# A two-block transformer kernel: first norm's squares moved to ScalarE on a natural copy of the input, residual squares one tile behind, two sets of products moved behind the first tiles

## The chip, the cores and the metric

The kernel runs on one core of a Trainium2 chip. The time is the device time of one execution in microseconds; the time of a kernel is the median of its runs. Beside the runs stands one profiled execution, from whose trace all rows below are taken.

## The reference, cut to what matters

256 tokens of width 2048 in fp32 go through a first block (a double attention, then a gated feed-forward part) and a second block (an attention layer, then a retention layer).

```python
def rms_norm(x, g):
    xf = x.astype(jnp.float32)
    y = xf * lax.rsqrt(jnp.mean(xf * xf, axis=-1, keepdims=True) + NORM_EPS)
    return (y * g.astype(jnp.float32)).astype(x.dtype)

# first block
u = rms_norm(h, norm_pre_mix)
proj = u @ w_in                      # 256 x 2048 @ 2048 x 8512
...
mixed = (g_sb * y_sb + g_mla * y_mla) @ w_out
h = h + rms_norm(mixed, norm_post_mix)
gu = rms_norm(h, norm_pre_ffn) @ w_gate_up
h = h + rms_norm((silu(g) * up) @ w_down, norm_post_ffn)
# second block, layer 0: attention with normed and rotated q and k
q = apply_rope(rms_norm_2(q, q_gain), cos, sin) * (A_HEAD_DIM ** -0.5)
k = apply_rope(rms_norm_2(k, k_gain), cos, sin)
p = softmax(q @ k.T); o = p @ v; y = (o * silu(gate)) @ w_out
# then a residual layer norm, the retention layer and a second residual layer norm
```

## The kernel before, in words

**Units.** All weights stream through one loop (`run`, line 226). A unit is one tile of weights of 256 x 512: SP's queue loads it into `raw` (five buffers, four units ahead in the order written), ScalarE copies it into the high part `whi`, VectorE subtracts to give the low part `wlo` (four buffers, split three units ahead), and TensorE uses both with the high and low parts of the activations, three products for each pair. `gemm_t` makes results transposed (features on partitions), `gemm_n` makes them natural (tokens on partitions), 512 columns a group, in two of the four PSUM banks of the pool `psg`. The pool hands its banks out in turn, so a group takes the banks of the group before the last. Every engine runs its own instructions in the order in which the program writes them.

**Background stages.** Work that is not a product of the stream (norms, attention heads, transposes) is cut into stages and put into tasks (`bg_add`). After each unit `bg_step` runs one stage that is due, or up to two in the attention layer (`rate` 2); at most two tasks are taken from the waiting list, `urgent` ones go ahead of them, `gap` is the least number of units between two stages, and `after` names a group that has to be finished first.

**The start.** The input comes transposed (`xs`, eight loads of two chunks between the first weight loads). `x_split` makes `u`'s high and low parts for two chunks ahead of each of the first eight weight splits, and has GpSimd square the chunks and add the squares up (`sq0`). After the first group, `r0_stages` sums `sq0` over partitions with TensorE (`token_sums`), computes the reciprocal root in small steps on GpSimd (`rms_bg`), spreads it over partitions and evacuates the first group (`evac_first`).

**The norm turns.** Between the output projection `w_out` and the feed-forward part the step `enter_ffn` ends one norm and begins the next matrix. The last group's two accumulators are read by a square on ScalarE (`sum_wout`) and by `put_wout`, two VectorE multiplications for each half of the tokens. `enter` turns the first tile of the new activations (transposes on TensorE, high part, low part); `two_groups` then interleaves the first two groups of the new matrix (unit order a0 a1 b0 b1 a2 a3 b2 b3 and so on), holds a0's products back until a1, and puts the seven other tile turns (`turn_now`) and the sums that they need (`turn_make`) behind certain units. The background task "h" meanwhile forms the residual `y` tile by tile on VectorE and squares each tile on ScalarE (`rest`). `enter_attn` does the same between `w_down` and the attention layer, with `put_down` (one VectorE multiplication for each half, in SBUF) and without squares. `b1` is the fourth unit of the interleaved order; its split is written in a0's place, and a2's behind a1.

**Attention.** `evac_qk` puts up a task "prep" for each group of four query heads: squares, rotation on VectorE and GpSimd, and a last stage `s3` of transposes and splits into `qT`. The heads' tasks (`att_head`) wait for the end of that task; their first stage multiplies `qT` with `kT`.

Of the kernel before, what the change touches and what calls it, by code (L numbers as in the profile page):

```python
# [10 lines left out]
F32 = mybir.dt.float32  # L11
# [3 lines left out]
ALU = mybir.AluOpType  # L15
AX = mybir.AxisListType

P = 128
S = 256
D = 2048  # L20
# [39 lines left out]
def tile_two_blocks(ctx: ExitStack, tc: tile.TileContext, a, out):  # L60
    nc = tc.nc
    pe, act, dve, pool = nc.tensor, nc.scalar, nc.vector, nc.gpsimd
# [3 lines left out]
    mp = ctx.enter_context(tc.tile_pool(name="main", bufs=1))  # L66
# [17 lines left out]
    def bbank():  # L84
        return psb.tile([P, 512], F32, tag="b", name="b")
# [23 lines left out]
    def mul(o, x, y, eng=None):  # L109
        tt(o, x, y, ALU.mult, eng)  # L110

    def add(o, x, y, eng=None):
        tt(o, x, y, ALU.add, eng)
# [10 lines left out]
    def stt(o, x, s, y, op0, op1):  # L124
        dve.scalar_tensor_tensor(out=o, in0=x, scalar=s, in1=y, op0=op0, op1=op1)  # L125
# [25 lines left out]
    def bg_add(group, stages, gap=2, after=None, delay=0, urgent=False):  # L151
        t = Task(group, stages, gap, after, clock[0] + delay)
        if urgent:
            active.insert(0, t)
        else:
            waiting.append(t)
# [66 lines left out]
    before_load, before_split = {}, {}  # L223
# [223 lines left out]
    def cols(g):  # L447
        return slice(g * 512, (g + 1) * 512)
# [6 lines left out]
    def square_sum(junk, x, acc):  # L455
        act.activation(out=junk, in_=x, func=AF.Square, accum_out=acc)  # L456
# [39 lines left out]
    def enter(high_on, chain, rest):  # L496


        new_u()
        tr, high, low = turning["fs"][0, 0]  # L500
        tr()
        high(high_on)
        chain()
        turning["make"](0, 1)
        low()
        for f in rest:
            f()
# [10 lines left out]
    def token_sums(ps, col, tiles, start=True, stop=True):  # L518

        for i, t in enumerate(tiles):  # L520
            for tb in range(2):
                mm(ps[:, col + tb:col + tb + 1], t[:, tb * P:(tb + 1) * P], ones[:, 0:1],
                   start and i == 0 and tb == 0, stop and i == len(tiles) - 1)

    def small(name, w=2, bufs=2):
        return mp.tile([P, w], F32, tag="sm_" + name, name=name, bufs=bufs)
# [16 lines left out]
    def rms_bg(key, get_ps, n, dst):  # L543

        st = {}

        def row():
            v, t = small("v"), small("t")
            st["r"] = small("r", bufs=6)
            ts(v, get_ps()[:, 0:2], 1.0 / n, ALU.mult, NORM_EPS, ALU.add)  # L550
            rsqrt_bg(st["r"], v, t)

        def wide():
            st["d"] = diag(st["r"], 1.0, "gate" if key == "kv" else "sqt")

        def use():
            o = bbank()
            spread(o, 0, st["d"])
            dst(key, st["r"], o[:, 0:S])
        return [row, nop, wide, use]  # L560
# [20 lines left out]
    p1 = open_phase("p1")  # L581
    xs = p1.tile([P, KD, S], F32, tag="c", name="xs")
# [4 lines left out]
    ifr = p1.tile([64, 64], F32, tag="ifr", name="ifr")[:, 0:2]  # L587
    nc.scalar.dma_start(out=cv, in_=a["cv"])
    pool.memset(f32(wz), 0.0)
    sq0 = p1.tile([P, 2, S], F32, tag="gate", name="sq0")  # L590

    copy(small("root"), f32(wz)[:, 0:2])
    warm(22)
# [12 lines left out]
        nc.sync.dma_start(out=kp, in_=a["kc"][:, 2 * P:7 * P])  # L606
    before_load[9] = const_load

    def x_split(c):
        def f():  # L610
            for k in (c, c + 1):
                copy(U[0][:, k, :], xs[:, k, :], scale=vec("pre_mix", k))
                stt(U[1][:, k, :], xs[:, k, :], vec("pre_mix", k), f32(U[0][:, k, :]), ALU.mult, ALU.subtract)
            if c == 0:
                mul(sq0, xs[:, 0:2, :], xs[:, 0:2, :], pool)
            else:
                s2 = p1.tile([P, 2, S], F32, tag="sqt", name="sqt")
                mul(s2, xs[:, c:c + 2, :], xs[:, c:c + 2, :], pool)
                add(sq0, sq0, s2, pool)
        return f  # L620
    for i in range(8):
        before_split[i] = x_split(2 * i)
# [6 lines left out]
        rows[key], bcast[key] = r, b  # L629

    def r0_stages(evac):
        st = {}

        def sums():
            st["ps"] = bbank()
            token_sums(st["ps"], 0, [sq0[:, 0, :], sq0[:, 1, :]])
        return [sums] + rms_bg("x", lambda: st["ps"], D, to_bcast) + [evac]


    tabs = {}  # L640
# [453 lines left out]
    fin = {}  # L1094
# [23 lines left out]
    def put_wout(g, tb, p):  # L1118
        y = fin["y"][:, tb, cols(g)]
        mul(y, p, fin["post_mix"][:, cols(g)])  # L1120
        mul(fin["yg"][tb][:, cols(g)], y, fin["pre_ffn"][:, cols(g)], pool if g < 3 else dve)
# [22 lines left out]
    def rms_last(tb):  # L1144
        v = small("v1", 1)
        stt(v, fin["ss"][:, 4 * tb + 3:4 * tb + 4], 1.0 / D, fin["s3"][:, tb:tb + 1], ALU.mult, ALU.add)
        rstd(fin["r"][:, tb:tb + 1], v)
# [16 lines left out]
    for g in range(4):  # L1164
        gemm_n(a["w_out"], KD, g * 512, 512, u_rhs,
               lambda ps, g=g: [evac_wout(g, tb, p) for tb, p in enumerate(ps)],
# [1 line left out]
    at_unit(len(units) - 2, before_end)  # L1168

    def enter_ffn():  # L1170
        enter(dve, lambda: rms_last(1), [lambda tb=tb: put_wout(3, tb, fin.pop(("p", tb))) for tb in range(2)])
        fin["h"], fin["ss2"] = fin["y"], small("ss", 8)

        def rest(c, tb):
            def f():
                y = fin["y"][:, tb, cols(c)]
                stt(y, y, fin["r"][:, tb:tb + 1], fin["x"][:, tb, cols(c)], ALU.mult, ALU.add)
                junk = p1.tile([P, 512], F32, tag="sqt", name="sqh")
                square_sum(junk, y, fin["ss2"][:, 4 * tb + c:4 * tb + c + 1])
            return f  # L1180
        bg_add("h", [nop] + [rest(c, tb) for c in range(4) for tb in range(2)], gap=1)

    step(enter_ffn, norm=True)


# [80 lines left out]
    def put_down(g, tb):  # L1266
        y = ffn["acc"][:, tb, cols(g)]
        mul(y, y, fin["post_ffn"][:, cols(g)], pool if g < 3 else dve)
# [31 lines left out]
    at_unit(len(units) - 2, before_end)  # L1300

    def enter_attn():
        enter(dve, lambda: rms_last(1), [lambda tb=tb: put_down(3, tb) for tb in range(2)])

    step(enter_attn, norm=True)

# [23 lines left out]
    def evac_qk(n, g):  # L1330
        def evac(ps):
            if not at:
                start_attn()
            p3 = at["p"]
            raw = p3.tile([P, 2, 512], F32, tag="raw", name="qkraw", bufs=2)
            for tb in range(2):
                copy(raw[:, tb, :], ps[tb])
            st = {}
            tab = at["tab"][n]

            def s1():
                sq = p3.tile([P, 2, 512], F32, tag="qsq", name="qsq")
                act.activation(out=sq, in_=raw, func=AF.Square)
                v, r, t = small("v8", 8), small("r8", 8), small("t8", 8)
                dve.tensor_reduce(out=v, in_=sq.rearrange("p a (h d) -> p (a h) d", d=P), axis=AX.X, op=ALU.add)
                ts(v, v, 1.0 / P, ALU.mult, NORM_EPS, ALU.add)
                rsqrt_bg(r, v, t)
                st["r"] = r

            def s2(tb):  # L1350
                def fn():
                    if tb == 0:
                        st["t"] = p3.tile([P, 2, 512], F32, tag="qsq", name="qt2")
                    t = st["t"]
                    q4 = raw[:, tb, :].rearrange("p (h d) -> p h d", d=P)
                    mul(q4, q4, st["r"][:, 4 * tb:4 * tb + 4, None].to_broadcast([P, 4, P]))
                    for qt in range(2):
                        def qv(x, which):
                            return x[:, tb, :].rearrange("p (h f w d) -> p h f w d", h=4, f=2, w=2)[:, :, :, which, :]
                        sn = tab[:, 1, tb, :].rearrange("p (f w d) -> p f w d", f=2, w=2)[:, :, qt, :]  # L1360
                        mul(qv(t, qt), qv(raw, 1 - qt), sn[:, None, :, :].to_broadcast([P, 4, 2, 32]))
                    mul(q4, q4, tab[:, 0, tb, None, :].to_broadcast([P, 4, P]), pool)
                    add(raw[:, tb, :], raw[:, tb, :], t[:, tb, :], pool)
                return fn

            def s3():
                dst = p3.tile([P, 2, 4, S], F32R, tag=n + "T", name=n + "T", bufs=2 if n == "q" else 1)
                for j in range(2):
                    o = bbank()
                    for i in range(4):  # L1370
                        h, tb = 2 * j + i // 2, i % 2
                        pe.transpose(out=o[:, i * P:(i + 1) * P], in_=raw[:, tb, h * P:(h + 1) * P], identity=ident)
                    split_psum(dst[:, 0, 2 * j:2 * j + 2, :], dst[:, 1, 2 * j:2 * j + 2, :], split2(o))
                at[n, g] = dst
            wait = [nop, nop] if n == "q" else [nop] * 6
            bg_add("prep%s%d" % (n, g), [s1, nop, s2(0), s2(1), nop, nop] + wait + [s3], gap=1, urgent=True)
        return evac

    def evac_av(ps):
# [427 lines left out]
```

## Time and profile before

| | us |
|---|---|
| median of three runs | 2552.85 |
| lowest and highest | 2552.61, 2554.2 |
| profiled execution, its own time | 2553.11 |
| its span in the trace | 2551.4 |

The profiled execution lies 0.26 us above the median, and 1.7 us of it lie outside the span. TensorE is busy in almost the whole span, so what matters is where it stands still and where its clock is not at full speed. A row of a timeline gives the start, the duration, the engine, the line of the kernel (often that of a helper, so that the tile's name says more), the operation and tiles, the count, and in brackets the engine's idle time before it with the instruction that ended that time.

### The profile page before, as it was taken

The numbers are of one execution on the slowest core, as the hardware profiler recorded it, in microseconds if no ns is written. First come the engines' busy times: TensorE is split into PE (matmuls) and PEld (weight loads), VectorE is DVE, ScalarE is ACT, GpSimd is POOL, SyncE is SP. The second block draws the span as 40 slices with busy tenths as digits, with TensorE's granted clock in tenths as the row PEclk, the third lists the DMA queues.
The fourth block names the chain that finished last, engine by engine and source line by source line (L and its number), as shares of the span: only waits on it lengthen the run. The fifth ranks groups of instructions, "written<-read, shape, count | busy, mean of one in ns | idle before, by whom it ended". The sixth has DMA issues, their size and how long they took to land.

```text
span 2551.4 us, 36111 instructions
## 1 busy us (share of the span) xinstructions
PE 2496.5 (98%) x14332; PEld 2181.9 (86%) x14332; DVE 1518.1 (60%) x1794; ACT 1191.9 (47%) x1478; POOL 237.6 (9%) x348
## 2 busy tenths in 40 slices
PE   8999999999899999999999999999999999999997
PEld 8999999998678888888888788887989898898786
DVE  7756666556655454444555676766775656565545
ACT  4565554444444444444444455543444454454332
POOL 4012000002000000000000031112010110102000
PEclk9999999999999999999999999999999999999998
DMA  7555556656466666666656555455756556665763
GB/s 234 175 162 165 167 163 197 227 179 196 144 189 185 191 188 190 195 191 190 186 184 199 156 186 153 149 192 172 227 163 183 167 180 182 178 184 154 261 192 120
DMA packets 248890, 465.49 MB, mean 182 GB/s; under 512 B 21328, under 2 KB 31888, under 8 KB 247696
## 3 DMA queue, kind: packets, MB, share of 16 engines
q1 hardware_dynamic: 244736, 447.28, 57.8%
q0 software_dynamic: 2688, 13.63, 1.4%
q8 instruction: 112, 1.84, 0.3%
q10 hardware_dynamic: 1296, 2.27, 0.2%
q14 instruction: 58, 0.48, 0.1%
HBM read 458.92 MB, written 4.19 MB: 182 GB/s over the span
## 4 chain that ended last, share of the span: by engine, by line
PE 88%; DVE 6%; ACT 2%; issue 2%; DMA 1%; POOL 1%; SPq 0%; ACTq 0%; DVEq 0%; POOLq 0%
PE g L101 83%; PE b L101 4%; DVE wlo L107 2%; ACT whi L104 1%; DMA raw<-in_ret_w_out_dram 1%; POOL t L107 1%; DVE u L107 0%; DVE h L125 0%; PE b L1239 0%; DMA raw<-in_w_in_dram 0%; POOL t L433 0%; PE b L466 0%; DVE y L125 0%; DVE qkraw L107 0%; PE b L1661 0%
## 5 line engine op out<-in xcount | busy, mean ns | idle before, releaser
L107 DVE TENSOR_TENSOR wlo<-raw,whi 128x1024 fp32r<-128x1024 f32 (+2 forms) x849 | 1061.6, 1259 | 790.6 <-ACT whi L104 786.0
L104 ACT ACTIVATE whi<-raw 128x1024 fp32r<-128x1024 f32 (+2 forms) x852 | 887.2, 1050 | 869.7 <-PE g L101 825.6
L101 PE MATMUL g<-whi,u 128*128 128x512 f32 x3200 | 1013.3, 393 | 11.9 <-DVE u L107 4.7
L101 PEld LDWEIGHTS g<-whi,u 128*128 128x128 f32 x3200 | 602.5, 189 | 141.1 <-DVE u L107 7.6
L101 PE MATMUL g<-wlo,u 128*128 128x512 f32 x1600 | 626.0, 391 | 2.1 <-DVE wlo L107 2.0
L101 PE MATMUL g<-u,whi 128*128 128x256 f32 x3424 | 601.2, 280 | 1.3 <-ACT whi L104 1.2
L101 PEld LDWEIGHTS g<-u,whi 128*128 128x128 f32 x3424 | 520.3, 188 | 2.5 <-ACT whi L104 1.7
L101 PE MATMUL g<-u,wlo 128*128 128x256 f32 x1712 | 476.8, 279 | 8.0 <-DVE wlo L107 8.0
L101 PEld LDWEIGHTS g<-wlo,u 128*128 128x128 f32 x1600 | 302.1, 189 | 64.0 <-DVE wlo L107 3.2
L101 PEld LDWEIGHTS g<-u,wlo 128*128 128x128 f32 x1712 | 322.2, 188 | 10.2 <-DVE wlo L107 10.2
L101 PE MATMUL g<-whi,mh 128*128 128x512 f32 x352 | 139.0, 395 | 0.0
L101 PE MATMUL g<-whi,ml 128*128 128x512 f32 x352 | 137.0, 392 | 0.0
L101 PE MATMUL g<-wlo,mh 128*128 128x512 f32 x352 | 136.7, 388 | 0.0
L101 PE MATMUL g<-wlo,roh 128*128 128x512 f32 x256 | 100.6, 393 | 1.7 <-DVE wlo L107 1.7
L101 PE MATMUL g<-whi,roh 128*128 128x512 f32 x256 | 99.9, 390 | 0.1
L101 PE MATMUL g<-whi,rol 128*128 128x512 f32 x256 | 98.5, 394 | 0.0
L107 POOL TENSOR_TENSOR t<-r 128x2 f32<-128x2 f32 (+1 forms) x51 | 22.0, 431 | 633.5 <-DVE r L122 630.9
L101 PEld LDWEIGHTS g<-whi,ml 128*128 128x128 f32 x352 | 66.1, 188 | 15.4
L101 PEld LDWEIGHTS g<-wlo,mh 128*128 128x128 f32 x352 | 66.1, 188 | 14.6
L101 PEld LDWEIGHTS g<-whi,mh 128*128 128x128 f32 x352 | 66.2, 188 | 13.1
L107 POOL TENSOR_TENSOR dacc<-dacc,post_ffn 128x512 f32<-128x512 f32 x6 | 7.7, 1300 | 657.6 <-ACT sqd L456 657.6
L101 PEld LDWEIGHTS g<-wlo,roh 128*128 128x128 f32 x256 | 48.0, 188 | 13.8 <-DVE wlo L107 2.8
(315 smaller groups left out, 2221.3 us busy)
## 6 DMA issues: line engine op xcount, KB each, us to landing
raw<-in_ret_w_in_dram SPq DMA_DIRECT2D x192, 512.0 KB, 4.3
raw<-in_w_gate_up_dram SPq DMA_DIRECT2D x176, 512.0 KB, 3.7
raw<-in_w_in_dram SPq DMA_DIRECT2D x128, 512.0 KB, 4.5
raw<-in_w_down_dram SPq DMA_DIRECT2D x88, 512.0 KB, 4.5
raw<-in_attn_w_in_dram SPq DMA_DIRECT2D x80, 512.0 KB, 3.6
raw<-in_ret_w_out_dram SPq DMA_DIRECT2D x64, 512.0 KB, 4.6
raw<-in_w_out_dram SPq DMA_DIRECT2D x32, 512.0 KB, 4.4
raw<-in_attn_w_out_dram SPq DMA_DIRECT2D x32, 512.0 KB, 4.5
```

The lines of the kernel that those rows point to most:

```text
L101: pe.matmul(out=o, lhsT=l, rhs=r, start=start, stop=stop, skip_group_check=True)
L104: act.activation(out=o, in_=i, func=AF.Copy, **k)
L107: (eng or dve).tensor_tensor(out=o, in0=x, in1=y, op=op)
```

## The change

The first norm's squares are taken from a natural copy of the input (`x0`, 2 MB, tokens on partitions), which GpSimd's queue loads, by two ScalarE instructions that square and add up a row of 2048 (stages 1 and 2 of `r0_stages`, which becomes one stage longer); GpSimd's squares and sums in `x_split` and TensorE's `token_sums` go. In `enter_ffn` the four multiplications of `put_wout` for the last chunk leave the step and become the first two stages of the task "h"; in the stages after them the square of a residual tile is written one stage behind the tile. In `enter_attn` the two multiplications of `put_down` for the last chunk become a task of their own, behind units a1 and b0. In `evac_qk` each prep task gets an empty last stage.

```diff
--- before.py
+++ after.py
@@ -587,7 +587,8 @@
     ifr = p1.tile([64, 64], F32, tag="ifr", name="ifr")[:, 0:2]
     nc.scalar.dma_start(out=cv, in_=a["cv"])
     pool.memset(f32(wz), 0.0)
-    sq0 = p1.tile([P, 2, S], F32, tag="gate", name="sq0")
+    x0 = mp.tile([P, 2, D], F32, tag="x", name="x0")
+    ss0 = small("ss0")
 
     copy(small("root"), f32(wz)[:, 0:2])
     warm(22)
@@ -606,17 +607,15 @@
         nc.sync.dma_start(out=kp, in_=a["kc"][:, 2 * P:7 * P])
     before_load[9] = const_load
 
+    def x0_load():
+        pool.dma_start(out=x0, in_=a["x"].rearrange("(b p) c -> p b c", p=P))
+    before_load[8] = x0_load
+
     def x_split(c):
         def f():
             for k in (c, c + 1):
                 copy(U[0][:, k, :], xs[:, k, :], scale=vec("pre_mix", k))
                 stt(U[1][:, k, :], xs[:, k, :], vec("pre_mix", k), f32(U[0][:, k, :]), ALU.mult, ALU.subtract)
-            if c == 0:
-                mul(sq0, xs[:, 0:2, :], xs[:, 0:2, :], pool)
-            else:
-                s2 = p1.tile([P, 2, S], F32, tag="sqt", name="sqt")
-                mul(s2, xs[:, c:c + 2, :], xs[:, c:c + 2, :], pool)
-                add(sq0, sq0, s2, pool)
         return f
     for i in range(8):
         before_split[i] = x_split(2 * i)
@@ -629,12 +628,9 @@
         rows[key], bcast[key] = r, b
 
     def r0_stages(evac):
-        st = {}
-
-        def sums():
-            st["ps"] = bbank()
-            token_sums(st["ps"], 0, [sq0[:, 0, :], sq0[:, 1, :]])
-        return [sums] + rms_bg("x", lambda: st["ps"], D, to_bcast) + [evac]
+        def sums(tb):
+            return lambda: square_sum(x0[:, tb, :], x0[:, tb, :], ss0[:, tb:tb + 1])
+        return [sums(0), sums(1)] + rms_bg("x", lambda: ss0, D, to_bcast) + [evac]
 
 
     tabs = {}
@@ -1168,17 +1164,25 @@
     at_unit(len(units) - 2, before_end)
 
     def enter_ffn():
-        enter(dve, lambda: rms_last(1), [lambda tb=tb: put_wout(3, tb, fin.pop(("p", tb))) for tb in range(2)])
+        enter(dve, lambda: rms_last(1), [])
         fin["h"], fin["ss2"] = fin["y"], small("ss", 8)
 
-        def rest(c, tb):
+        items = [(c, tb) for c in range(4) for tb in range(2)]
+
+        def rest(i):
+
             def f():
-                y = fin["y"][:, tb, cols(c)]
-                stt(y, y, fin["r"][:, tb:tb + 1], fin["x"][:, tb, cols(c)], ALU.mult, ALU.add)
-                junk = p1.tile([P, 512], F32, tag="sqt", name="sqh")
-                square_sum(junk, y, fin["ss2"][:, 4 * tb + c:4 * tb + c + 1])
+                if i < 8:
+                    c, tb = items[i]
+                    y = fin["y"][:, tb, cols(c)]
+                    stt(y, y, fin["r"][:, tb:tb + 1], fin["x"][:, tb, cols(c)], ALU.mult, ALU.add)
+                if i:
+                    c, tb = items[i - 1]
+                    junk = p1.tile([P, 512], F32, tag="sqt", name="sqh")
+                    square_sum(junk, fin["y"][:, tb, cols(c)], fin["ss2"][:, 4 * tb + c:4 * tb + c + 1])
             return f
-        bg_add("h", [nop] + [rest(c, tb) for c in range(4) for tb in range(2)], gap=1)
+        puts = [lambda tb=tb: put_wout(3, tb, fin.pop(("p", tb))) for tb in range(2)]
+        bg_add("h", puts + [rest(i) for i in range(9)], gap=1)
 
     step(enter_ffn, norm=True)
 
@@ -1300,7 +1304,8 @@
     at_unit(len(units) - 2, before_end)
 
     def enter_attn():
-        enter(dve, lambda: rms_last(1), [lambda tb=tb: put_down(3, tb) for tb in range(2)])
+        enter(dve, lambda: rms_last(1), [])
+        bg_add("put", [nop] + [lambda tb=tb: put_down(3, tb) for tb in range(2)], gap=1)
 
     step(enter_attn, norm=True)
 
@@ -1372,8 +1377,8 @@
                         pe.transpose(out=o[:, i * P:(i + 1) * P], in_=raw[:, tb, h * P:(h + 1) * P], identity=ident)
                     split_psum(dst[:, 0, 2 * j:2 * j + 2, :], dst[:, 1, 2 * j:2 * j + 2, :], split2(o))
                 at[n, g] = dst
-            wait = [nop, nop] if n == "q" else [nop] * 6
-            bg_add("prep%s%d" % (n, g), [s1, nop, s2(0), s2(1), nop, nop] + wait + [s3], gap=1, urgent=True)
+            wait = [nop] * (2 if n == "q" else 6)
+            bg_add("prep%s%d" % (n, g), [s1, nop, s2(0), s2(1), nop, nop] + wait + [s3, nop], gap=1, urgent=True)
         return evac
 
     def evac_av(ps):
```

## Rows read from the trace of the kernel before

**Rows 1.** The page's part 1: busy time, share, instructions of each engine.

```profile
PE 2496.5 (98%) x14332; PEld 2181.9 (86%) x14332; DVE 1518.1 (60%) x1794; ACT 1191.9 (47%) x1478; POOL 237.6 (9%) x348
```

**Rows 2.** Waits of TensorE over the whole span: us in total, times, longest.

```profile
PE g L101 <- DVE wlo L107: 12.5, 13, 3.0
...
PE b L101 <- ACT qT L104: 2.8, 4, 0.8
...
PE b L101 <- DVE qT L107: 0.9, 4, 0.2
```

**Rows 3.** Windows of the start: us, five engines' busy time, granted clock, DMA, GB/s.

```profile
0.00:14.00 14.00, 8.55 (x54) 7.95 (x55) 8.54 (x7) 9.39 (x16) 8.94 (x11) 1.00 0.88 309
14.00:18.00 4.00, 3.83 (x22) 3.53 (x20) 4.00 (x4) 3.18 (x6) 3.76 (x4) 0.57 0.98 359
18.00:30.00 12.00, 8.71 (x71) 8.31 (x72) 12.00 (x9) 3.88 (x7) 9.92 (x7) 1.00 0.59 169
```

**Rows 4.** Timeline of the start, TensorE.

```profile
6.64 2.10 PE L101 MATMUL g<-u,whi 128*128 128x256 f32 x16 [1.19 <-ACT whi L104]
...
13.29 0.39 PE L101 MATMUL g<-u,wlo 128*128 128x256 f32 x1 [3.00 <-DVE wlo L107]
...
41.04 0.95 PE L101 MATMUL b<-kc,sq 128*128 128x1 f32 x8
```

**Rows 5.** Timeline of the start, VectorE.

```profile
13.16 2.68 DVE L125 SCALAR_TENSOR_TENSOR u<-xs,cv,u 128x256 fp32r<-128x256 f32 x2
...
30.13 0.87 DVE L125 SCALAR_TENSOR_TENSOR u<-xs,cv,u 128x256 fp32r<-128x256 f32 x2
30.92 1.21 DVE L107 TENSOR_TENSOR wlo<-raw,whi 128x1024 fp32r<-128x1024 f32 x1
```

**Rows 6.** Timeline of the start, ScalarE.

```profile
5.53 1.06 ACT L104 ACTIVATE whi<-raw 128x1024 fp32r<-128x1024 f32 x1 [0.65 <-DMA raw<-in_w_in_dram]
...
38.40 1.06 ACT L104 ACTIVATE whi<-raw 128x1024 fp32r<-128x1024 f32 x1 [1.65 <-PE g L101]
```

**Rows 7.** DMA, 436.5 to 447: queues (packets, MB, share); issue (KB, us to landing).

```profile
q0 software_dynamic: 348, 2.72, 62.6%
q1 hardware_dynamic: 593, 1.15, 35.3%
...
xres<-in_x_dram POOLq DMA_DIRECT2D x1, 2048.0 KB, 9.5
```

**Rows 8.** ScalarE's copies of input chunks: ns min/median/max, first and last start.

```profile
L104 ACT ACTIVATE u<-xs,cv x16: 492/492/508, 4.0 to 22.1; 128x256 fp32r<-128x256 f32 x16
```

**Rows 9.** Windows of two norm turns, columns as in rows 3.

```profile
662.24:710.81 48.57, 39.52 (x169) 29.92 (x170) 32.63 (x42) 21.59 (x36) 2.91 (x1) 0.96 0.42 120
1416.91:1454.69 37.78, 37.65 (x169) 30.45 (x170) 27.15 (x32) 16.68 (x20) 2.88 (x1) 0.95 0.57 167
```

**Rows 10.** Timeline of the norm before the feed-forward block, TensorE.

```profile
662.24 0.47 PE L101 MATMUL g<-whi,u 128*128 128x512 f32 x1 [0.88 <-DVE v L125]
...
670.00 2.50 PE L101 MATMUL g<-whi,u 128*128 128x512 f32 x5 [2.25 <-DVE u L107]
```

**Rows 11.** Timeline of the same norm, VectorE, then ScalarE.

```profile
664.60 0.68 DVE L107 TENSOR_TENSOR y<-g,post_mix 128x512 f32<-128x512 f32 x1
665.32 1.57 DVE L107 TENSOR_TENSOR yg<-y,pre_ffn 128x512 f32<-128x512 f32 x1
...
668.13 1.22 DVE L107 TENSOR_TENSOR wlo<-raw,whi 128x1024 fp32r<-128x1024 f32 x1
669.26 0.68 DVE L107 TENSOR_TENSOR u<-b,u 128x512 fp32r<-128x512 f32 x1
...
671.26 1.06 ACT L104 ACTIVATE whi<-raw 128x1024 fp32r<-128x1024 f32 x1 [5.83 <-PE g L101]
```

**Rows 12.** Waits in that norm's turn, 664 to 708, all engines.

```profile
ACT sqh L456 <- DVE y L125: 17.8, 8, 3.3
```

**Rows 13.** Timeline of one attention group, TensorE.

```profile
1616.00 0.38 PE L101 MATMUL g<-u,wlo 128*128 128x256 f32 x1 [0.54 <-DVE wlo L107]
```

## The prediction

> **What bounds the kernel.** I read the page first. TensorE is busy for 98% of the span [rows 1], so the time is its matrix work plus the places where it stands still or runs at half clock; no other engine is near its limit over the whole. A faster ScalarE or GpSimd is worth nothing by itself. The second view is TensorE's waits over the whole span. The ones that the change can touch are its waits for `wlo`, most of them in the start, and for `qT` in the attention [rows 2]. The third view is the table of windows over the start, then the timelines of the start, of the norm before the feed-forward block and of one attention group, and the DMA view at the one place where a 2 MB load on GpSimd's queue already runs beside the weights.
>
> **The start: what goes.** From 4 to 28 us GpSimd squares and adds almost without a pause, and VectorE is full from 14 to 30 [rows 3]. VectorE's two products for a pair of chunks take 2.68 us while GpSimd works and 0.87 when it has stopped [rows 5]. With the subtraction (1.21 undisturbed) a unit needs 2.1 us of VectorE without GpSimd and over 4 with it, against TensorE's 2.72 for a unit (ScalarE's 1.06 and its 1.65 of waiting for TensorE to give a buffer back [rows 6]). So in the start VectorE sets the pace, and TensorE waits: 3.0 us at 13.29 alone [rows 4]. It then runs at a granted clock of 0.57 from 14 to 18 us [rows 3], which lies near the lower level of 1.2 GHz, after standing still before 13.29; that costs 4 x 0.43 = 1.7 us. With GpSimd's 15 instructions gone, VectorE needs less than TensorE.
>
> The pace is then TensorE's, and the question is when it begins. Before, the first weights were there at 5.53 and the products began at 6.64 [rows 4, 6]; 16 of unit 0's 24 products took 2.10, so it ended near 9.75, and unit 8 at 41.04, where the eight token sums begin [rows 4]. If nothing else changed, unit 8 would end at 9.75 + 8 x 2.72 = 31.5, 9.5 us earlier. The token sums go too: 0.95 us with the overlap into the next product, of which I count 0.8.
>
> **The start: what comes.** The 2 MB of `x0` are written into the program at the ninth load, but GpSimd's queue holds nothing in front of them except the first memset, and their buffer has no earlier reader. They start at about 1.1 us, in the window in which the DMA engines are already full (share 0.88 over 0 to 14 with its first 2 us empty, 0.98 from 14 to 18) [rows 3]. The nearest rows are those of the other 2 MB load on this queue: 9.5 us to landing, with 62.6% of the engines' time against 35.3% for the weights' queue beside it [rows 7]. With about 390 GB/s for the whole, the weights' queue gets 0.138 MB/us while `x0` flows, from about 2.7 to 10.6 us. The first input chunks (0.26 MB) are through by then, the 0.52 MB of the first weights need 3.8 us, and with 1 us to the semaphore (before: 0.79 MB from 2.0 on, seen at 5.5) they are there at 7.5. TensorE begins at 8.6, takes 3.1 us for unit 0, and has stood still from about 5.5 on, longer than before 13.29; I charge the same 1.7 us of half clock. Unit 0 ends at 13.4. The data of unit 1 (1.57 MB in all) are complete near 12.2 and split at 14.5, so it loses 1.0. Unit 8 ends at 14.4 + 21.8 = 36.2 instead of 41.04: 4.8, and with the token sums 5.6 us. Bounds: if all of `x0` goes ahead of the first weights, these land near 13, unit 8 ends at 40.6, and 1.2 us are left; if `x0` hinders nothing it is 9.5 + 0.8 = 10.3.
>
> The Trainium skill, "DMA: Bandwidth & Descriptors", section "Queues, rings and completion order", says that an engine alternates between the queues that have work, a whole packet at a time, which speaks against this load. The trace's shares, 62.6 to 35.3, are milder than a strict alternation of its packets would make them; by that rule the sum would be 15.8 us, by the shares 17.7. What alternation would do here stands among the rivals, from rows.
>
> ScalarE pays two squares of 2048. From 492 ns for 256 [rows 8] and 1.06 us for 1024 [rows 6] I get 0.74 ns an element, so 1.8 us each, 2.0 with reading the sum. They stand in units 8 and 9, where ScalarE waits 1.65 us for TensorE in every unit [rows 6]; 0.35 us is too much each time, and the next `whi` behind them is late by 0.7 us at most. Splits run three units ahead (8.2 us), so nobody waits: 0. The chain has one stage more, so the first group is evacuated behind unit 14 instead of 13; its banks are wanted at unit 16, one unit remains, and the cost is 0. If that cover went, each us of lateness would cost one.
>
> **The norm before the feed-forward block.** The two turns have the same transposes and the same kind of products. From the first use of the new activations to the last transposes the one takes 48.57 us and TensorE is busy for 39.52; the other, which has no squares in its background task, takes 37.78 and is busy for 37.65 [rows 9]. So 10.8 us are there to be had. 2.25 of them are one wait for the low part of tile (0,1) [rows 10]: in front of it VectorE does the four multiplications for the last chunk, from 664.60 to about 668.1 [rows 11]. The rest is a chain between two engines: in each of eight units ScalarE's square waits for VectorE's residual tile (17.8 us in all [rows 12]), the `whi` stands behind the square, `wlo` waits for that `whi`, and the next tile comes behind `wlo`. With the square one stage behind its tile, ScalarE no longer waits; VectorE's unit (1.22 + 0.68 + 0.74 for the residual) fits into TensorE's.
>
> The change doesn't take all of it. Written as the first stage of "h", `put_wout` of the first half is still in front of the low part (a0's stage comes before a1's turn). VectorE then does b1's `wlo` (1.22, about 0.9 longer because GpSimd's subtraction of the step disturbs one instruction, as it now makes 1.57 of a 0.68 [rows 11]), two multiplications and the low part: ready near 668.6 instead of 669.9, so 0.9 us of the wait stay. `put_wout` of the second half goes behind a2's `wlo`, and this is a new wait: its first multiplication frees the PSUM bank that b0 wants for its second half of tokens. TensorE would resume at 668.65, use a0's `whi` for the last time at 669.1; ScalarE's a2 `whi` starts 0.34 later (now 1.26 after 670.00, with two products at half clock [rows 10, 11]), and 1.06 + 1.22 + 0.68 follow: the bank is free at 672.5. TensorE wants it at 668.65 + 4 x 0.23 + 6 x 0.23 = 670.9: it stands 1.6 us, with all later products behind it. New length: 37.78, less 0.28 for that turn's own small wait at its low part, plus 0.9 + 1.6 = 40.0; gain 8.6 us. Bounds: 10.8 if neither wait comes; 4.5 if both come, the clock halves again behind them (1.7) and a third of the chain's waits stays (2.4).
>
> **The attention turn.** Two multiplications (0.68 each) leave VectorE's way ahead of the same low part. TensorE is idle for 0.13 us in this whole turn [rows 9], with another 0.15 hidden in the modelled ends. They touch no PSUM, and land behind units in which VectorE has room. 0.3 us, from 0 to 0.6.
>
> **The attention heads.** TensorE waits 2.8 + 0.9 us, eight times in four groups, for `qT` [rows 2]: the first head's scores run in the same unit as the splits that they need. The empty last stage keeps the group pending, so they run a unit later. Each group's heads end one unit later; the last low part of all is then forced ahead of the products for chunks 12 and 13, while its own is used a unit later: 0. But a head's scores now share a unit with the next group's square and reduction, and in that stretch TensorE already waits 0.54 us for `wlo` [rows 13], in three groups. I take 3.7 - 0.5 = 3.2 us; bounds 0.7 (three waits longer by 1 us) and 5.3 (those go too).
>
> **Sum.** 5.6 + 8.6 + 0.3 + 3.2 = 17.7 us. Against the profiled execution: 2553.11 - 17.7 = 2535.4; against the median, which lies 0.26 lower, 2535.2.
>
> **Rivals, and how the numbers follow.** 0.2% is 5.1 us, about what a measurement of this kernel can tell from no change.
>
> The sum as it stands has a chance of 0.40.
>
> Strict alternation of packets in the start: the rows give 2.72 MB in 348 packets and 1.15 MB in 593 [rows 7], 7.8 and 1.9 KB, so `x0` would take four fifths. The first weights would need 6.7 us instead of 3.8 and unit 1 no longer waits: the start gives 3.7, the time is 2537.1. Against it stand the shares measured; but there the weights' queue was not full all the time. 0.17.
>
> The norm's turn keeps its standstill: the bank's wait and 1.7 us of half clock behind it, with some of the chain: gain there 4.9, time 2538.9. 0.18.
>
> The prep stage doesn't do what it should: the wait for `qT` comes back as waits for `wlo`, gain 0.7 there, time 2537.7. 0.13.
>
> `x0` is hidden wholly: 2530.5. 0.07.
>
> Slower: ScalarE takes its work in order, so a square of `x0` that waits for its data holds every later `whi`. It is reached near 33 us; with 8.2 us of splits ahead, each us of landing after about 41 costs one. The load would have to land after 59 to undo the 17.7, and after 64 to make the kernel slower by 0.2% (2558). By rows 7 it lands near 10.6. 0.02. Several terms failing at once, so that under 5.1 us remain: 0.03.
>
> Faster 0.95, same 0.03, slower 0.02. The ends of the terms add up to 6.4 and 27.2 us; all at one end is unlikely. The range leaves about 2 in 10 out: 2528 to 2544.
>
> **What would show it.** In the start: no GpSimd work, VectorE's pairs at 0.9, the first products at 8 to 10 us, unit 8 at its end near 36. In the norm's turn: squares that wait for nothing, a wait of about 1.6 us in b0 released by the multiplication on VectorE, 40 us in all. In the attention: no wait for `qT`. The prediction is wrong if the first weights land after 10 us, if the two turns stay over 4 us apart, or if waits for `wlo` grow in the attention.

## The result, and the profile after

The kernel after takes 2524.55 us (median of 4 runs, 2523.39 to 2526.17) against 2553.32 for the kernel before on the same chip (4 runs, 2552.61 to 2554.2): ratio 0.9887, 95% interval 0.9875 to 0.99, a gain of 28.8 us. Forecast were 17.7 us and 2535.2, with a range of 2528 to 2544. The direction was right, the gain was 11 us larger than the sum, and the time lies below the range.

The waits of TensorE over the whole span of the kernel after, columns as in [rows 2]:

```profile
PE g L101 <- ACT whi L104: 6.5, 3, 4.9
PE g L101 <- DVE wlo L107: 4.5, 7, 1.4
...
PE g L101 <- DVE u L107: 2.3, 2, 1.7
...
PE b L466 <- DVE z L125: 1.6, 1, 1.6
```

No wait for `qT` is left, and the waits for `wlo` fell from 12.5 us in 13 places to 4.5 in 7 [rows 2]. A new one stands at the top: 4.9 us for a `whi` of ScalarE. It lies in the start, as the windows show (columns as in [rows 3]):

```profile
0.00:14.00 14.00, 8.15 (x46) 7.65 (x46) 3.00 (x5) 4.74 (x8) 1.39 (x6) 0.98 0.87 321
14.00:18.00 4.00, 2.80 (x11) 2.51 (x12) 3.29 (x5) 3.77 (x7) 0.00 (x0) 0.50 1.07 400
18.00:30.00 12.00, 12.00 (x96) 12.00 (x95) 9.85 (x15) 8.95 (x14) 0.00 (x0) 0.91 1.06 395
```

GpSimd hardly works in the start and VectorE is no longer full, as forecast. But from 14 to 18 us the granted clock is 0.50, the lower of the two levels (1.2 of 2.4 GHz), all the time, and 0.91 from 18 to 30. The timeline of TensorE says where that comes from:

```profile
6.71 2.15 PE L101 MATMUL g<-u,whi 128*128 128x256 f32 x16 [0.48 <-ACT whi L104]
...
14.73 0.80 PE L101 MATMUL g<-u,whi 128*128 128x256 f32 x2 [4.93 <-ACT whi L104]
15.99 0.58 PE L101 MATMUL g<-u,wlo 128*128 128x256 f32 x1 [0.46 <-DVE wlo L107]
```

Unit 0 begins at 6.71, as early as before (6.64, [rows 4]); unit 1 waits 4.93 us for its data, and TensorE comes out of that standstill at half clock. The DMA view from 5 to 10 us names the cause (packets, MB, share of the 16 engines, then the load of `x0`, issued by 1.4 us, with its time to landing in the view from 0 to 12):

```profile
q0 software_dynamic: 215, 1.76, 87.6%
q1 hardware_dynamic: 212, 0.22, 12.5%
```

```profile
x<-in_x_dram POOLq DMA_DIRECT2D x1, 2048.0 KB, 11.0
```

The two queues pass the same number of packets, 215 and 212. Those of `x0` carry 8.2 KB each (1.76 MB by 215), those of the input chunks on the weights' queue 1.0 KB, so the weights' queue gets an eighth of the engines' time. The Trainium skill, "DMA: Bandwidth & Descriptors", section "Queues, rings and completion order", says that an engine alternates between its queues by whole packets; these rows agree (215 to 212).

The windows of the two norm turns, from the first use of the new activations to the last transposes, as in [rows 9]:

```profile
655.51:694.82 39.31, 36.46 (x169) 29.21 (x169) 32.78 (x42) 21.75 (x36) 2.91 (x1) 1.00 0.54 158
1398.91:1436.22 37.31, 37.31 (x169) 30.41 (x169) 27.07 (x32) 16.68 (x20) 2.90 (x1) 0.95 0.57 170
```

The first was 48.57 us and is 39.31, forecast 40.0; the second was 37.78 and is 37.31. Both waits that the working named are there, together nearly at their size (1.65 and 1.19 for 0.9 and 1.6), and no half clock follows them (granted 1.00):

```profile
662.67 1.43 PE L101 MATMUL g<-whi,u 128*128 128x512 f32 x5 [1.65 <-DVE u L107]
...
666.42 0.50 PE L101 MATMUL g<-whi,u 128*128 128x512 f32 x1 [1.19 <-DVE y L107]
```

**What no term names.** I matched the matmuls of the two traces in their order and took the difference of their starts, the lead of the kernel after (and, further down, of the other runs, always against the kernel before). It is 1.4 us at 230 us; it grows by 5.3 us from there to the norm's turn, by 2.25 in the feed-forward block and by 1.3 and 1.4 in the output projections of the attention and of the retention: 10.3 us together. No edit touches these stretches, and TensorE hardly waits in them. The groups of TensorE's instructions by shape show what differs: the same instructions, in the same number, take less time each (count, then busy us and mean ns of one). The kernel before:

```profile
L101 PE MATMUL g<-whi,mh 128*128 128x512 f32 x352 | 139.0, 395 | 0.0
...
L101 PE MATMUL g<-whi,ol 128*128 128x512 f32 x128 | 49.8, 397 | 0.0
...
L101 PE MATMUL g<-omh,whi 128*128 128x256 f32 x128 | 36.1, 282 | 0.0
```

And the kernel after:

```profile
L101 PE MATMUL g<-whi,mh 128*128 128x512 f32 x352 | 137.4, 390 | 0.0
...
L101 PE MATMUL g<-whi,ol 128*128 128x512 f32 x128 | 48.9, 390 | 0.0
...
L101 PE MATMUL g<-omh,whi 128*128 128x256 f32 x128 | 35.5, 277 | 0.0
```

In these groups a matmul of 512 columns takes 5 to 7 ns less, one of 256 columns 5 ns less; from start to start `omh` with `whi` goes from 119.4 to 114.1 ns. All groups that gained read one tile of a phase's pool (`lath`, `osb`, `omh`, `mh`, `oh`, `roh` and their low parts), though not every group that does gained: `wlo` with `mh` takes 388 ns before and 389 after. Products of `u` with the weights, whose tiles lie in other pools, have the same mean before and after in the stretch from 452 to 640 us (276 and 390 ns). What the change did to the phase tiles is in no line that the prediction looked at: the new small tile `ss0` (2 buffers of 32 bytes) lies below the phase pools in SBUF and pushes them up by 64 bytes. In the built programs the tiles named begin 192 bytes past a multiple of 256 before the change, and on a multiple of 256 after it. `u`, `whi` and `wlo` begin on a multiple of 256 in both.

### The profile page after: what moved, and what is told of

Its sections match the earlier page's. It is cut to its first block, busy times and chain, and to the rows that moved or that the text cites. A ratio compares the mean times of both kernels' runs of the same rounds, so it can differ in the third digit from the quotient of the medians.

```text
span 2524.5 us, 36073 instructions
## 1 busy us (share of the span) xinstructions
PE 2481.5 (98%) x14324; PEld 2177.9 (86%) x14324; DVE 1506.9 (60%) x1794; ACT 1195.4 (47%) x1482; POOL 216.2 (9%) x334
## 4 chain that ended last, share of the span: by engine, by line
PE 91%; DVE 4%; ACT 2%; DMA 1%; issue 1%; POOL 1%; SPq 0%; ACTq 0%; DVEq 0%; POOLq 0%
PE g L101 86%; PE b L101 4%; DVE wlo L107 1%; ACT whi L104 1%; DMA raw<-in_ret_w_out_dram 1%; DVE h L125 0%; DMA raw<-in_w_in_dram 0%; PE b L466 0%; PE b L1243 0%; POOL t L107 0%; DVE u L107 0%; ACT pp L1403 0%; PE b L1666 0%; PE b L1414 0%; DVE nm L1400 0%
```

## The experiments

**Theory A**: the place of the phase tiles sets how fast TensorE's matmuls follow each other, and this gave the 11 us that no term names. **Rival B**: those 11 us come from what the edits do on other engines. For the start: alternation of packets (theory) against a DMA path that is full anyway (rival).

The kernel before was timed again beside each group of runs, with medians of 2553.41 to 2554.55 us. The ratios below are to that median; a difference to the kernel after is one of medians, and by the ratios it comes out up to 1.2 us otherwise.

**The kernel before, phase pools 64 bytes higher.**

```diff
+    copy(small("ss0"), f32(wz)[:, 0:2])
```

> The kernel before, with one small tile more and a copy of two numbers into it: every tile of the phase pools lies 64 bytes higher, no instruction of the work is changed. Theory A (the place of the tiles in SBUF sets the spacing of the matmuls, and this made the part of the gain that no edit explains): the products of the first stage and of the attention's projections go from 118.8 to about 114.5 ns and from 231 to 227 ns, and the time falls by 8 to 12 us, to 2541 to 2545. Rival B (the spacing comes from what the edits do on the other engines): no spacing changes, 2553 within 2.

Measured: 2543.01 us against 2554.55, ratio 0.9954 (0.9942 to 0.9967). One dead copy of two numbers makes the tuned kernel 11.5 us faster. The same three groups:

```profile
L101 PE MATMUL g<-whi,mh 128*128 128x512 f32 x352 | 137.4, 390 | 0.0
...
L101 PE MATMUL g<-whi,ol 128*128 128x512 f32 x128 | 48.9, 389 | 0.0
...
L101 PE MATMUL g<-omh,whi 128*128 128x256 f32 x128 | 35.6, 278 | 0.0
```

They read as in the kernel after, to 1 ns. The differences of the means by the counts, over the twenty groups that read a phase tile, add up to 11.4 us, which is the whole gain. The same sum fits the three runs that follow: 10.0 us more for 128 bytes (9.9 by the medians), 2.2 more for 192 (2.2), 0.2 less for 256 (0.1).

**128 bytes higher.** Two such lines (`ss0`, `ss1`).

> The kernel before, with two such small tiles: the phase pools lie 128 bytes higher. Theory A in its narrow form (the position within 128 bytes counts): spacing and time of the kernel before, 2553 within 2. Theory A in a wide form (any other place is better than the old one): about 2543 as with 64 bytes. Rival B: 2553.

Measured: 2564.40, ratio 1.0038 (1.0026 to 1.0051), 10 us slower than before. Neither form of A had said this; B is excluded once more. The tiles now begin 64 past a multiple of 256:

```profile
L101 PE MATMUL g<-whi,mh 128*128 128x512 f32 x352 | 139.5, 396 | 0.0
...
L101 PE MATMUL g<-whi,ol 128*128 128x512 f32 x128 | 49.5, 394 | 0.0
...
L101 PE MATMUL g<-omh,whi 128*128 128x256 f32 x128 | 36.3, 283 | 0.0
```

So the period isn't 128 bytes. The next two tell whether it is 256.

**192 bytes higher.** Three such lines.

> The kernel before with three such small tiles: the phase pools lie 192 bytes higher, at 128 from a multiple of 256 (before: 192, with 64 more: 0, with 128 more: 64). If the position within 256 bytes sets the spacing and 0 is the good one by itself, this is slower than before or near it, 2548 to 2565. If only 0 and 128 are good (multiples of 128), 2543 within 2.

Measured: 2555.61 against 2553.41, ratio 1.0007 (0.9998 to 1.0017). At 128 past a multiple of 256 the kernel is as slow as before: of the four places tried only the multiple of 256 is fast.

```profile
L101 PE MATMUL g<-whi,mh 128*128 128x512 f32 x352 | 139.4, 396 | 0.0
...
L101 PE MATMUL g<-whi,ol 128*128 128x512 f32 x128 | 49.6, 395 | 0.0
...
L101 PE MATMUL g<-omh,whi 128*128 128x256 f32 x128 | 35.7, 279 | 0.0
```

**256 bytes higher.** Four such lines.

> The kernel before with four such small tiles: the phase pools lie 256 bytes higher, so at the same position within 256 bytes as before. If that position is all that counts: 2553 within 2, products of the first stage near 118.8 ns. If a longer period or the mere distance counts: another time.

Measured: 2553.31 against 2553.41, ratio 0.9998 (0.9989 to 1.0008), and these groups are those of the kernel before to the last digit:

```profile
L101 PE MATMUL g<-whi,mh 128*128 128x512 f32 x352 | 139.0, 395 | 0.0
...
L101 PE MATMUL g<-whi,ol 128*128 128x512 f32 x128 | 49.8, 397 | 0.0
...
L101 PE MATMUL g<-omh,whi 128*128 128x256 f32 x128 | 36.1, 282 | 0.0
```

This run is also the control for the added copies: four of them cost and gain nothing.

**The kernel after, with the phase pools where they were.**

```diff
-    ss0 = small("ss0")
+    ss0 = small("s3")
```

> The kernel after, with the tile for the sums of squares taken from a small tile that exists already, so that the phase pools lie where they lay before. Theory A: the spacing goes back to 118.8 and 231 ns, the edits alone are left with about 2553.3 - 17 = 2536, 8 to 12 us slower than after. Rival B: 2524.5 within 2.

Measured: 2535.73, ratio 0.9926 (0.9913 to 0.9938); 11.2 us slower than after (10.0 by the ratios). The three groups read as in the kernel before again (395, 397 and 282 ns). These are the edits alone, and the forecast for them was 2535.2.

**The load of `x0` behind eight loads on the weights' queue.**

```diff
-        pool.dma_start(out=x0, in_=a["x"].rearrange("(b p) c -> p b c", p=P))
+        nc.sync.dma_start(out=x0, in_=a["x"].rearrange("(b p) c -> p b c", p=P))
```

> The kernel after, with the load of x0 on the queue of the weights, behind eight loads, instead of on a queue of its own. Theory: the packets of x0 no longer alternate with those of the second chunk pair, its data land near 8 instead of 12.5 us, the 4.9 us of standing still and most of the 6.8 us at half clock go, and the time falls by 5 to 9 us, to 2516 to 2520. Rival: the bytes are the same and the queues are full until about 30 us, so the wait only moves to a later unit: within 2 us of after, 2524.5.

Measured: 2517.21, ratio 0.9854 (0.9839 to 0.9869), 7.3 us faster than after. The windows of its start:

```profile
0.00:14.00 14.00, 11.36 (x75) 10.96 (x76) 7.28 (x12) 9.61 (x16) 0.52 (x5) 1.00 0.87 310
14.00:18.00 4.00, 4.00 (x38) 4.00 (x37) 3.94 (x7) 3.71 (x7) 0.00 (x0) 1.00 1.06 397
18.00:30.00 12.00, 12.00 (x108) 12.00 (x107) 5.97 (x8) 4.21 (x6) 0.00 (x0) 1.00 1.04 400
```

The same bytes at the same rate (310 to 400 GB/s in both), but the clock is whole and TensorE hardly stands still (its longest waits are 0.75 and 0.72 us, before unit 0 and in unit 1): unit 9 begins at 32.75 us, 40.33 in the kernel after. The rival is excluded: what counted was the order of the bytes, not their number.

**Squares of the norm back in the stage of their tiles** (`rest`):

```diff
-                if i:
-                    c, tb = items[i - 1]
...
-        bg_add("h", puts + [rest(i) for i in range(9)], gap=1)
+        bg_add("h", puts + [rest(i) for i in range(8)], gap=1)
```

> The kernel after with each square of the norm before the feed-forward block back in the stage of its residual tile. Theory (the chain between ScalarE and VectorE is what the turn loses): the squares wait again, some 10 to 18 us in all, the turn is 7 to 8 us longer, 2531.5 to 2533. Rival (the turn's gain comes from moving the last chunk's multiplications): at most 2 us longer, 2524.5 to 2526.5.

Measured: 2532.84, ratio 0.9921 (0.9904 to 0.9937), 8.3 us slower than after. In its trace the turn's gain falls from 9.3 us of lead to 0.1. The squares wait as in [rows 12], where it was 17.8 us:

```profile
ACT sqh L456 <- DVE y L125: 18.6, 8, 3.3
```

**The last chunk's multiplications of that norm back in the step:**

```diff
-        enter(dve, lambda: rms_last(1), [])
+        enter(dve, lambda: rms_last(1), [lambda tb=tb: put_wout(3, tb, fin.pop(("p", tb))) for tb in range(2)])
...
-        bg_add("h", puts + [rest(i) for i in range(9)], gap=1)
+        bg_add("h", [nop, nop] + [rest(i) for i in range(9)], gap=1)
```

> The kernel after with the last chunk's four multiplications of that norm back in front of the low part of the first new tile; the squares stay a stage behind. Theory: the wait for the low part is 2.2 to 2.8 us again instead of 1.65, the wait for the bank (1.2) goes, half a clock behind it may come back (1.7): from 1 us faster to 1.5 us slower than after, 2523.5 to 2526. Rival (moving them is what counts): 5 us slower or more, 2529.5.

Measured: 2524.18, ratio 0.9883 (0.9868 to 0.9897): the same as after. The wait for the low part is 2.3 us again and the bank's wait is gone; the half clock that might come back did (granted 0.66 over the 5 us behind that wait), and the turn gives 8.5 us of lead in this trace instead of 9.3. Moving `put_wout` exchanged one wait for another and is worth nothing by the medians; the square behind its tile is the whole gain of that turn.

**Without the empty last stage of a prep task** (`evac_qk`):

```diff
-            bg_add("prep%s%d" % (n, g), [s1, nop, s2(0), s2(1), nop, nop] + wait + [s3, nop], gap=1, urgent=True)
+            bg_add("prep%s%d" % (n, g), [s1, nop, s2(0), s2(1), nop, nop] + wait + [s3], gap=1, urgent=True)
```

> The kernel after without the empty last stage that holds a group's heads back by a unit in the attention. Theory (that stage gave the whole gain in the heads, 5.3 us once the placement is taken out): the eight waits for qT come back, 3.7 us in all, and 2524.5 + 4 to 5.5 = 2528.5 to 2530. Rival (part of those 5.3 us came from elsewhere): 2524.5 + 2 to 3.5.

Measured: 2531.19, ratio 0.9911 (0.9897 to 0.9926), 6.6 us slower than after, a little over what was expected; the products of the two traces differ by 5.9 us in the heads. The waits of [rows 2] are back, 3.5 us in all; in what else the 5.9 lie isn't shown:

```profile
PE b L101 <- ACT qT L104: 2.6, 4, 0.8
...
PE b L101 <- DVE qT L107: 0.9, 4, 0.2
```

**The last chunk's multiplications back in the turn to the attention** (the two of `put_down` in the step, no task "put"; the expectation counts four).

> The kernel after with the four multiplications of the last chunk back in front of the low part in the turn to the attention. Forecast of this edit: 0.3 us; the trace with the old placement showed 1.2. So 2524.8 to 2526. Rival: nothing, 2524.5, as TensorE hardly stood idle there.

Measured: 2524.86, ratio 0.9889 (0.9874 to 0.9903). 0.3 us by the medians, which these runs can't tell from nothing. Its trace has a wait of 1.5 us for the low part in that turn, which the kernel after has not.

**The banks freed first in the norm's turn:**

```diff
-        puts = [lambda tb=tb: put_wout(3, tb, fin.pop(("p", tb))) for tb in range(2)]
+        ys = [lambda tb=tb: mul(fin["y"][:, tb, cols(3)], fin.pop(("p", tb)), fin["post_mix"][:, cols(3)]) for tb in range(2)]
+        ygs = [lambda tb=tb: mul(fin["yg"][tb][:, cols(3)], fin["y"][:, tb, cols(3)], fin["pre_ffn"][:, cols(3)]) for tb in range(2)]
+        puts = [lambda: [f() for f in ys] and None, lambda: [f() for f in ygs] and None]
```

> The kernel after with the two multiplications that free the PSUM banks of the last chunk in the first stage of that norm's task and the two that follow from them in the second. Theory: the wait for the bank (1.2 us) goes and the wait for the low part stays 1.65: 2523.3 within 1. Rival: the two multiplications come in front of the same low part and make it later by as much: no change.

Measured: 2522.38 (2521.23 to 2525.33), ratio 0.9878 (0.9862 to 0.9895). The bank's wait is gone from the trace, the wait for the low part is 1.5 us, and the lead in that turn grows by 1.5; the intervals of the two kernels overlap.

**Both: `x0` on the weights' queue and the banks first.**

> The kernel after with x0 on the queue of the weights and the banks freed first. By the sum of the single edits: 7.3 + 1.2 us less than after, 2516 within 1.5.

Measured: 2517.50 (2515.36 to 2518.51), ratio 0.9856 (0.9841 to 0.9871). That is the time of the kernel with `x0` moved alone (0.9854): the second edit adds nothing that can be measured, though its trace has 1.6 us in that turn again. The version to keep is the one with the single moved line, 37 us under the kernel before.

## Why the prediction was right and wrong

The trace of the edits alone (phase pools where they were) gives each term in the place where it was forecast (us):

| term | forecast | lead gained there |
|---|---|---|
| start | 5.6 | 2.3 |
| norm before the feed-forward block | 8.6 | 9.2 |
| turn to the attention | 0.3 | 1.2 |
| heads | 3.2 | 5.3 |
| sum | 17.7 | 18.0 |

That the two sums agree is in part luck: the start gave 3.3 us less than forecast, the three other terms 3.6 more.

**The step that failed** is the sum itself, "5.6 + 8.6 + 0.3 + 3.2 = 17.7 us": it went over instructions, waits and transfers, and took for granted that a matmul that the change doesn't touch keeps its price. About 11 us came from the matmuls' price. This is shown: the shift alone gives 11.5 us on the kernel before, and taking it out costs 11.2 on the kernel after (10.0 by the ratios). No rival named it, and even all terms at their upper ends (27.0 us; the working adds them up to 27.2) don't reach the measured 28.8. What could have been seen blind: the diff adds a tile to a pool that lies below others, and the trace of before has the products of the phase tiles at 118.7 ns from start to start and those of `u` at 113.5 in the same stretch (300 to 560 us). That is a hint and no proof: in other stretches of the same trace those of `u` take 117.8 themselves.

**The start was mis-sized**, 2.3 and not 5.6 us (1.4 in the kernel after). The beginning of unit 1 was forecast at 14.4 and came at 14.73, which is luck, for it came by another way. The working had the weights' queue at 0.138 MB/us from 2.7 us on, and so unit 0 late; in fact only 16 packets of `x0` pass before 5 us, unit 0 is on time, and from 5 to 10 us the weights' queue gets 0.044 MB/us (0.22 in 5). The rival of strict alternation was right about the sharing, and its 3.7 us were nearer. What made the rest lies behind unit 1's beginning: unit 8 ended at 40.33, forecast 36.2. The 1.7 us of half clock were charged ahead of unit 1; it came behind the standstill, on the path. Units 1 to 8 take 25.6 us, eight of the later ones (2.82 each) 22.6; of the difference the wait at 15.99 is 0.46 and the half clock about 2.5. And a unit took 2.82 us where the working had 2.72, 0.8 for the eight. With the one line moved the lead is 8.8 us at 230 us, near the 10.3 of the bound "if `x0` hinders nothing".

**The norm's turn** went as worked out: both waits in their places, 39.31 us for 40.0, and the chain between ScalarE and VectorE as the cause (with the squares back in their stages 8.3 us are lost by the medians, and all but 0.1 of the gain in the trace). The rival in which half a clock stays behind the bank's wait didn't happen.

**The turn to the attention** gave 1.2 us in the trace of the edits alone, 0.5 in that of the kernel after, and 0.3 by the medians. The 1.2 can't be put down to the edit: before and after run part of that turn at half clock (granted 0.95 over the turn), the edits alone don't (1.00).

**The heads** gave the upper bound, 5.3: the three waits for `wlo`, 1.6 us in that stretch of the kernel before, were taken to grow by 0.5, and they went (0.2 is left in the trace of the edits alone). The rival in which they grow was wrong. That the empty stage removed them isn't shown: the trace without it has none of the three either, while products of `u` follow each other more slowly there (117.3 ns, before 114.3). The reason why the group's square and reduction don't collide with the scores was not tested.

**ScalarE** squares `x0` in 1.90 us each at 38.55 and 41.40, forecast 1.8, and nobody waits for it.

## What to carry to other kernels

Before a sum over instructions, look whether the change moves a tile: where the same matmul has two prices in one trace, compare where its operands begin, and try one dummy tile in the pool below. A second queue is no free way for a load while the first is full; where queues alternate by packets, the one with the larger packets takes the engines, so put a big load that nobody needs soon on the same queue, behind what is needed first. Where a background stage hands a tile from one engine to the next, let the second engine work a stage behind.

## What the runs showed of the hardware

The price of a matmul in fp32 depended on where its tile begins in SBUF, and 256 bytes more gave the same price again: on a multiple of 256 the products of `omh` and `whi` follow each other in 114.6 ns, at 64 past one in 120.4, at 128 in 118.2, at 192 in 119.4; those of `whi` and `mh` in 226.8, 233.1, 233.4 and 231.6 (means over the group, steps over 0.3 us left out). `wlo` with `mh` went with it at 64 and 128 (233.5 and 233.2) but not at 192 (226.0, and 226.7 on the multiple). Only these four places were tried, with all phase tiles moved together and the weights on multiples of 256; why it is so stays open.

There is a second effect that I can't explain. Products of `u` and the weights, whose tiles never moved, follow each other at either 113.3 or 117.8 ns, and change over from one stretch to another. In the start of the kernel after a unit of 24 products takes 2.83 us (the first product with `wlo` of a triple, and the one eight triples on):

```profile
20.43 0.28 PE L101 MATMUL g<-u,wlo 128*128 128x256 f32 x1
...
23.26 0.28 PE L101 MATMUL g<-u,wlo 128*128 128x256 f32 x1
```

and with `x0` on the weights' queue 2.72:

```profile
16.13 0.28 PE L101 MATMUL g<-u,wlo 128*128 128x256 f32 x1
...
18.85 0.28 PE L101 MATMUL g<-u,wlo 128*128 128x256 f32 x1
```

In the edits alone a unit takes 2.72 us as well. From 24 to 55 us this gives them 1.1 us over the kernel after, of which 0.6 make up for a later start; that is most of the difference between 1.4 and 2.3 us in the start.

The clock, too, did not do the same each time. Between the first groups of the feed-forward block TensorE waits 2.66 to 2.68 us for `sg` in all fourteen traces. In nine of them it then runs at half clock for a while (granted 0.79 over 8 us), in five it doesn't, and their lead grows by 1.3 to 1.4 us there. The kernel after, and the one with the squares back:

```profile
707.00:715.00 8.00, 5.98 (x21) 4.80 (x22) 2.89 (x4) 3.10 (x5) 1.53 (x6) 0.79 0.76 262
714.70:722.70 8.00, 5.97 (x28) 4.95 (x29) 4.23 (x5) 3.76 (x5) 1.53 (x6) 1.00 0.80 260
```

So a difference of this size between two traces proves nothing by itself. Both effects may be what spreads the runs of one kernel over 1 to 7 us; that wasn't tried.
